# Merged score groups, sliding values read at once, and float32 modulation sums in a decoder layer on one core

## The chip, the cores and the metric

The kernel runs on one core of one Trainium2 chip. A core has five engines that run their own instruction streams side by side and wait for each other by semaphores: PE (TensorE, matrix multiplication into PSUM), DVE (VectorE), ACT (ScalarE), POOL (GpSimd) and SP (SyncE, which here only issues DMAs). In the profile PEld is PE's loading of weights. PSUM has eight banks of 128 partitions by 512 float32 values, and each score or product has to be read out of its bank before the bank is used again.

The metric is the device time of one execution in microseconds, as the median of several executions. The profile is of one further execution; its own time and its span stand in the table below.

## The reference

One decoder layer on a sequence of 512 rows of 1024 values, in float32, cut to what matters here:

```python
mod = cs @ w_ada[l] + b_ada[l]                  # cs = silu(c), one row of 1024; mod has 6 rows of 1024
shift1, scale1, gate1, shift2, scale2, gate2 = split(mod, 6)
h = _rmsnorm(x, norm1_g[l]) * (1.0 + scale1) + shift1
qa, ka, va, qd, kd, vd, ga, gd = split(h @ w_in[l], points)
out_a = _sliding_window_attention(qa, ka, va, sinks, slopes)   # 8 heads, 2 key heads, window 128, blocks of 128
out_d = _diff_attention(qd, kd, vd, lam, ...)                  # 4 heads, softmax 0 minus lam times softmax 1, causal
merged = sigmoid(ga) * (out_a @ w_branch_swa[l]) + sigmoid(gd) * (out_d @ w_branch_diff[l])
x = x + gate1 * (merged @ w_out[l])
h2 = _rmsnorm(x, norm2_g[l]) * (1.0 + scale2) + shift2
x = x + gate2 * _conv_ffn(h2, ...)
return _rmsnorm(x, final_g)
```

The change touches three places: the scores of the two kinds of attention, the moment at which a sliding head's values are read out, and the last four rows of `mod` (gate1, shift2, scale2, gate2).

## The kernel before

**Precision.** A large product is made of three matmuls of fp32r operands (`mm3`, L118 to L121): each operand is split into a high part, rounded by ACT (`split`, L115), and a low part, the difference, made by DVE (L116); high times high, high times low and low times high are summed in one bank. `evac` does the same on the way out of a bank: ACT writes the high part (L430, or L433 with a scale), DVE the low part (L431, L434).

**PE's order is written out.** PE's instructions run in the order of the program text (`manual_schedule`, for PE alone). ACT, DVE, POOL and SP are ordered by a planner that simulates the program; where the text has `high_priority`, an instruction is taken as soon as it can run. So the order on those engines can change where only PE's text was touched.

**The fill.** Between the pieces of attention PE works on projections. `fill(n)` (L491) takes n steps from a list of units, a unit being one output block of 128 columns of a weight (q, k and v of a differential head, or a gate, or a branch), and a step three matmuls of 512 columns. The counts stand in `SWA_FILL` and `DIFF_FILL` (L37, L38). A weight comes by a DMA into one of four raw buffers (tag "raw", L105), is split, and then frees its raw buffer. `fill` also counts ticks: things put off by `after(n, ...)` run n ticks later, and every eighth tick the generator `ada_rows` goes one step.

**PSUM.** Two banks "f" for the fill, three "s" for scores, two "t" for transposes and other short uses, one "v" for the values of a head (L90 to L103).

**Sliding heads**, in four pairs i (heads i and i+4; j is 0 or 1). `swa_scores` (L532) makes the scores of four blocks n of 128 queries against 128 keys (block 0) or 256, two blocks at a time; the two j use the two halves of the array's rows, six matmuls for a block (`mm3_rows`, L126). DVE adds the window's bias and takes the maximum (L559). `swa_softmax` makes nm from the maxima (L570) and exponentials on ACT (es at L571, st at L574), and DVE divides (L582). `swa_transpose` (L593) turns the probabilities in the two "t" banks; ACT copies them out as pT (L595). `swa_values` (L604) multiplies by the values, the two j in the two halves of the array's columns, and `evac` (L609) writes outa with the planner's ordinary priority. Within a round i, the first two blocks of pair i+1 come ahead of the fill, the other two behind the second transpose of pair i, and the softmax of i+1 after one more fill.

**Differential heads**, in 16 steps s (head h, block n of 128 queries against (n+1) × 128 keys). `diff_scores` (L648 to L677) makes two maps m in the two halves of the rows; DVE adds the bias and takes the maximum (L673). Then nm (L685), exponentials (L687), the difference of the maps (L690 to L693), the transpose td (L702) and its `evac` to aTh and aTl (L705, L430, L431). `diff_values` (L709) makes od once in a head. Which scores are made at a step stands in `nxt`: blocks 0 and 1 together, 2 and 3 alone.

**Turning the values.** The values of a differential head come out transposed as vT (L632) and are turned by PE 13 ticks later (`turn`, pv, L637) into a "t" bank.

**The modulation rows.** `ada_rows` (L743) sums each of eight half rows (4 rows, 2 halves) over the input in blocks of two times 128: SP loads ra (L750) into a raw buffer, DVE multiplies by cs and sums into `arow` (L755 for the first, L757 for the other seven). All eight half rows use the one buffer "sq2". The sum over partitions follows on PE: `arow` is split into arh and arl, and a product with an all-ones 128x128 matrix puts the sum into every row of pr (L766, L767). ACT copies row 0 back into the same buffer (L769), and POOL's DMA puts it into DRAM (L770).

Of the kernel before, what the change touches and what calls it, by code (L numbers as in the profile page):

```python
# [53 lines left out]
def kernel(  # L54
# [78 lines left out]
    warm = cpool.tile([P, 1], F32, name="warm")  # L133
    nc.vector.memset(warm, 0.0)
    nc.scalar.activation(warm, warm, AF.Exp)
    onesr = cpool.tile([P, P], F32R, name="onesr")
    nc.vector.tensor_copy(onesr, ones)
    mhalf = cpool.tile([P, 4], F32, name="mhalf")
    nc.gpsimd.memset(mhalf, -0.5)
    qsc = cpool.tile([P, 4], F32, name="qsc")  # L140
# [388 lines left out]
    class Pair:  # L529
        pass  # L530

    def swa_scores(i, n0):  # L532
        if n0 == 0:
            c = pairs[i] = Pair()
            c.mx, c.nm, c.lsum, c.es = (
                ap.tile([P, 2, NT], F32, tag=t, bufs=2, name=f"{t}{i}") for t in ("mx", "nm", "lsum", "es")
            )
            c.sb = [ap.tile([P, 2, P], F32, tag="st0", bufs=2, name=f"st{i}_0")]
            c.sb += [ap.tile([P, 2, 256], F32, tag="st", bufs=ST, name=f"st{i}_{n}") for n in range(1, NT)]
            c.pT = []  # L540
        c = pairs[i]
        sps = [sbank(f"sw{i}_{n0}_{j}", (P, 2, 256)) for j in range(2)]
        for n in (n0, n0 + 1):
            w = P if n == 0 else 2 * P
            k0 = max(0, n - 1) * P
            qs, ks = slice(n * P, (n + 1) * P), slice(k0, k0 + w)
            mm3_rows([
                (
                    sps[j][:, n - n0, :w],
                    [qa[64 * j : 64 * j + 64, i, b, qs] for b in range(2)],  # L550
                    [ka[64 * j : 64 * j + 64, b, ks] for b in range(2)],
                )
                for j in range(2)
            ])
        for n in (n0, n0 + 1):
            w = P if n == 0 else 2 * P
            for j in range(2):
                with tc.high_priority(offset=HP):
                    c.last = nc.vector.tensor_tensor_reduce(  # L559
                        c.sb[n][:, j, :w], sps[j][:, n - n0, :w], dsw[:, 256 - w : 256], 1.0, -3e38, ALU.add, ALU.max,  # L560
                        c.mx[:, j, n : n + 1],
                    )

# [34 lines left out]
    def swa_values(i):  # L598
        o = vbank(f"oa{i}")
        for kb in (0, 2, 1, 3):  # L600
            w = P if kb == 3 else 2 * P
            for j in range(2):
                rows = slice(64 * j, 64 * j + 64)
                nc.tensor.matmul(  # L604
                    o[rows, kb * P : kb * P + w], va[:, kb, rows],
                    pairs[i].pT[j][:, kb * 256 : kb * 256 + w],
                    start=kb == 0, stop=kb == 3, tile_position=(0, 64 * j),
                )
        evac(outa[0][:, i], outa[1][:, i], o)  # L609


    heads = {}
# [35 lines left out]
    def diff_scores(*ss):  # L648
        ops = []
        for s in ss:  # L650
            h, n = divmod(s, NT)
            t = heads[h]
            w = (n + 1) * P
            if n == 0:
                firsts[h] = [sbank(f"sd{h}_{m}", (P, 2, 256)) for m in range(2)]
            sps = [firsts[h][m][:, n, :w] if n < 2 else sbank(f"sd{h}_{n}_{m}")[:, :w] for m in range(2)]
            mm3_rows([
                (
                    sps[m],
                    [t[64 * m : 64 * m + 64, b, n * P : (n + 1) * P] for b in range(2)],  # L660
                    [t[64 * m : 64 * m + 64, 2 + b, :w] for b in range(2)],
                )
                for m in range(2)
            ])
            ops.append((s, sps, w))
        for s, sps, w in ops:
            h, n = divmod(s, NT)
            mx = ap.tile([P, 2], F32, tag="dmx", bufs=3, name=f"dmx{h}_{n}")
            pm = []
            for m in range(2):  # L670
                st = ap.tile([P, w], F32, tag="st", bufs=ST, name=f"sd{h}_{n}_{m}")
                with tc.high_priority(offset=HP):
                    nc.vector.tensor_tensor_reduce(  # L673
                        st, sps[m], ddf[:, 512 - w : 512], 1.0, -3e38, ALU.add, ALU.max, mx[:, m : m + 1]
                    )
                pm.append(st)
            scored[s] = mx, pm  # L677
# [65 lines left out]
    def ada_rows():  # L743
        for idx in range(4):
            for hf in range(2):
                c0 = (2 + idx) * D + hf * S
                ac = big.tile([P, S], F32, tag="sq2", name=f"arow{idx}{hf}")
                for k in range(0, KT, 2):
                    r = raw_tile([P, 2, S], f"ra{idx}{hf}_{k}")
                    nc.sync.dma_start(r, wada[k * P : (k + 2) * P, c0 : c0 + S].rearrange("(a p) n -> p a n", p=P))  # L750
                    with tc.high_priority(offset=HP // 2) if tick[0] > ADA_EASY else ExitStack():
                        for a in range(2):
                            cc = cs[:, k + a : k + a + 1]
                            if k + a == 0:
                                nc.vector.tensor_scalar_mul(ac, r[:, a], cc)  # L755
                            else:
                                nc.vector.scalar_tensor_tensor(ac, r[:, a], cc, ac, ALU.mult, ALU.add)  # L757
                    yield
                ah = big.tile([P, S], F32R, tag="g2b0", name=f"arh{idx}{hf}")
                al = big.tile([P, S], F32R, tag="g2b1", name=f"arl{idx}{hf}")  # L760
                split(ah, al, ac)
                after(ADA_LAG, lambda idx=idx, hf=hf, ac=ac, ah=ah, al=al: ada_spread(idx, hf, ac, ah, al))

    def ada_spread(idx, hf, ac, ah, al):
        pr = tbank(f"pr{idx}{hf}")
        nc.tensor.matmul(pr, onesr, ah, start=True, stop=False)  # L766
        nc.tensor.matmul(pr, onesr, al, start=False, stop=True)  # L767
        row = ac[0:1, :]
        nc.scalar.copy(row, pr[0:1, :])  # L769
        nc.gpsimd.dma_start(mod_rows[idx : idx + 1, hf * S : (hf + 1) * S], row)  # L770


    pair_w = {}
# [29 lines left out]
    add_head(0)  # L803
    add_head(1)
    fill(SWA_FILL[0])
    swa_scores(0, 0)
    with tc.issue_after(pairs[0].last.ins):
        fill(SWA_FILL[1])
        swa_scores(0, 2)
    with tc.issue_after(pairs[0].last.ins):  # L810
        swa_softmax(0)
        fill(1)
# [2 lines left out]
        fill(SWA_FILL[2] - 1)  # L815
    for i in range(SWA_PAIRS):
        more = i + 1 < SWA_PAIRS
        if more:
            swa_scores(i + 1, 0)
        fill(SWA_FILL[3])  # L820
        swa_transpose(i, 0)
        fill(SWA_FILL[4])
        swa_transpose(i, 1)
        if more:
            swa_scores(i + 1, 2)
        fill(SWA_FILL[5])
        if more:
            swa_softmax(i + 1)
# [14 lines left out]
    for s in range(4 * DIFF_HEADS):  # L843
# [4 lines left out]
            add_gate_a(2)  # L848
            add_gate_a(3)
        fill(DIFF_FILL[1])  # L850
        nxt = {0: (), 1: (s + 1,), 2: (s + 1,), 3: (s + 1, s + 2)}[n] if s < 15 else ()
        if nxt:
            diff_scores(*nxt)
        fill(DIFF_FILL[2])
# [932 lines left out]
```

## Time and profile before

| | us |
|---|---|
| median of 3 runs | 706.98 (706.82 to 708.46) |
| the profiled execution's own time | 708.24 |
| its span in the trace | 705.4 |
| PE busy / DVE busy / ACT busy in the span | 685.0 / 578.4 / 383.9 |
| sliding attention on PE, first score group to last values | 61.5 to 116.8 |
| differential attention on PE, first scores to last values | 116.8 to 217.0 |
| modulation sums on PE (pr), first and last | 108.2 and 293.1 |

How to read it: a row of a timeline has the start in us from the span's beginning, the duration, the engine, the line, the operation, what it writes and reads by tile names, the partitions and elements, and how many equal instructions were merged into the row. A bracket gives the idle time ahead of it and whose event ended it. Matmuls overlap in the records (a record has 0.39 us where the next one starts 0.23 later), so prices on PE are taken from start to start. Rows on ACT and DVE overlap a little too.

### The profile page before, as it was taken

To read this page: it belongs to the slowest core of one execution; us is meant where nothing else is said; L and a number is where in the kernel's file an instruction comes from. 1 tells how busy PE (TensorE), PEld (TensorE's weight loads), DVE (VectorE), ACT (ScalarE), POOL (GpSimd) and SP (SyncE) were. 2 spreads that over 40 slices of the span, in tenths; PEclk is the share of its full clock that TensorE was granted. 3 is DMA by queue.
4 is the path that set the end of the run, shared out by engine and by line. 5 is a ranking of instruction groups with operands and counts; after the bars stand their busy time and mean duration, and the time that the engine had idled before them with its cause. 6 is when DMAs were issued, how large, how long until landed. Compare 5 with 4: busy or idle time off the path is not lost. (4 is left out here: it accounts for less than half of the span.)

```text
span 705.4 us, 11197 instructions
## 1 busy us (share of the span) xinstructions
PE 685.0 (97%) x4155; PEld 597.1 (85%) x4155; DVE 578.4 (82%) x1107; ACT 383.9 (54%) x676; POOL 82.2 (12%) x100
## 2 busy tenths in 40 slices
PE   6999999999999999999999999999999999999994
PEld 6777777777787888888889999999999999888884
DVE  5998968788985766773579899888888999979996
ACT  3646766545543333431468656555555666656664
POOL 3000000000011000000030111111101102530300
PEclk9999999999999999999999999999999999999998
DMA  9983624263543774529617888786979748996803
GB/s 311 302 262 98 201 61 154 67 199 90 170 153 100 262 214 142 186 93 288 187 33 148 197 199 204 177 209 182 208 204 230 164 143 204 197 200 191 158 0 119
DMA packets 115861, 121.80 MB, mean 173 GB/s; under 512 B 4415, under 2 KB 93280, under 8 KB 115808
## 3 DMA queue, kind: packets, MB, share of 16 engines
q1 hardware_dynamic: 96894, 95.09, 42.7%
q0 software_dynamic: 18720, 25.73, 21.6%
q8 instruction: 32, 0.52, 0.3%
q10 hardware_dynamic: 194, 0.28, 0.1%
q14 instruction: 21, 0.17, 0.1%
HBM read 118.97 MB, written 2.11 MB: 172 GB/s over the span
## 5 line engine op out<-in xcount | busy, mean ns | idle before, releaser
L1126 PE MATMUL up<-t,m_whi 128*128 128x256 f32 x528 | 96.1, 283 | 0.0
L1126 PEld LDWEIGHTS up<-t,m_whi 128*128 128x128 f32 x528 | 82.3, 192 | 0.0
L1126 PE MATMUL up<-t,m_wlo 128*128 128x256 f32 x264 | 74.7, 283 | 0.1
L1126 PE MATMUL up<-bh,p_wlo 128*128 128x256 f32 x232 | 65.7, 284 | 0.7 <-DVE p_wlo L1069 0.7
L1126 PE MATMUL up<-bh,p_whi 128*128 128x256 f32 x232 | 65.6, 283 | 0.0
L1126 PE MATMUL up<-bl,p_whi 128*128 128x256 f32 x232 | 65.6, 283 | 0.0
L1126 PEld LDWEIGHTS up<-t,m_wlo 128*128 128x128 f32 x264 | 50.6, 192 | 0.3 <-DVE m_wlo L1069 0.3
L1126 PEld LDWEIGHTS up<-bh,p_wlo 128*128 128x128 f32 x232 | 44.5, 192 | 1.1 <-DVE p_wlo L1069 1.1
L1126 PEld LDWEIGHTS up<-bh,p_whi 128*128 128x128 f32 x232 | 44.5, 192 | 0.0
L1126 PEld LDWEIGHTS up<-bl,p_whi 128*128 128x128 f32 x232 | 44.5, 192 | 0.0
L757 DVE SCALAR_TENSOR_TENSOR arow<-ra,cs,arow 128x512 f32<-128x512 f32 x56 | 41.9, 747 | 2.6 <-DMA ra<-in_w_ada_dram 1.8
L1037 POOL DMA_DIRECT2D s<-in_w_up_dram x21 | 27.0, 1361 | 142.9 <-DMA s<-in_w_up_dram 78.0
L1069 DVE TENSOR_TENSOR m_wlo<-s,m_whi 128x1024 fp32r<-128x1024 f32 x31 | 37.7, 1217 | 2.0 <-ACT m_whi L1065 2.0
L1065 ACT CAST m_whi<-s 128x1024 fp32r<-128x1024 f32 x31 | 32.5, 1047 | 9.4 <-DVE s L1059 5.9
L1126 PE MATMUL up<-t,p_whi 128*128 128x256 f32 x176 | 32.2, 283 | 0.0
L687 ACT ACTIVATE sd<-sd,dmx 128x128 f32<-128x128 f32 (+3 forms) x32 | 17.8, 556 | 23.2 <-DVE dmx L685 15.9
L175 POOL TENSOR_TENSOR r<-ms,mhalf 128x1 f32<-128x1 f32 (+1 forms) x16 | 13.2, 828 | 144.7 <-DVE ms L173 74.0
L1126 PEld LDWEIGHTS up<-t,p_whi 128*128 128x128 f32 x176 | 27.4, 192 | 0.2 <-issue 0.2
L1133 ACT ACTIVATE gT<-a,cv 128x512 f32<-128x512 f32 x22 | 17.7, 813 | 17.6 <-DVE a L1168 17.3
L770 POOL DMA_DIRECT2D mod_rows<-arow x8 | 4.3, 540 | 193.7 <-ACT arow L769 193.5
L1065 ACT CAST p_whi<-wa 128x1024 fp32r<-128x1024 f32 x18 | 18.7, 1041 | 12.0 <-PE up L1126 7.2
L1126 PE MATMUL up<-t,p_wlo 128*128 128x256 f32 x88 | 24.9, 283 | 0.0
(478 smaller groups left out, 2073.0 us busy)
## 6 DMA issues: line engine op xcount, KB each, us to landing
ra<-in_w_ada_dram SPq DMA_DIRECT2D x32, 512.0 KB, 4.2
wa<-in_w_up_dram SPq DMA_DIRECT2D x22, 512.0 KB, 4.6
s<-in_w_up_dram SPq DMA_DIRECT2D x21, 512.0 KB, 5.1
s<-in_w_up_dram POOLq DMA_DIRECT2D x21, 512.0 KB, 7.0
adaw<-in_w_ada_dram SPq DMA_DIRECT2D x16, 512.0 KB, 4.9
w<-in_w_in_dram SPq DMA_DIRECT2D x12, 512.0 KB, 4.1
a<-in_w_up_dram SPq DMA_DIRECT2D x11, 512.0 KB, 4.8
b<-in_w_down_dram SPq DMA_DIRECT2D x10, 512.0 KB, 4.7
```

Source lines behind the costliest of these rows:

```text
L175: nc.gpsimd.tensor_tensor(r0, ms, mhalf[:, :n], ALU.pow)
L687: nc.scalar.activation(pm[m], pm[m], AF.Exp, bias=mx[:, m : m + 1], scale=slope, accum_out=lsum[:, m : m + 1])
L757: nc.vector.scalar_tensor_tensor(ac, r[:, a], cc, ac, ALU.mult, ALU.add)
L770: nc.gpsimd.dma_start(mod_rows[idx : idx + 1, hf * S : (hf + 1) * S], row)
L1037: nc.gpsimd.dma_start(dst, upblock(*blk), accum_op=ALU.add)
L1065: nc.scalar.copy(W[J, name][0], R[J, SRC[name]])
L1069: nc.vector.tensor_sub(lo, R[J, SRC[name]], hi.bitcast(F32))
L1126: nc.tensor.matmul(o[u], w[:, k, cu], b[:, k], start=name in ("p1", "m5", "p2") and k == 0 and x == 0, stop=k == 3 and x == 2, skip_group_ ...
L1133: nc.scalar.activation(grow(j), av[J][:, u], AF.Identity, bias=cv[:, 66 + j : 67 + j], scale=cv[:, 44 + j : 45 + j])
```

## The change

Five edits.

1. The scores of sliding pairs 1 to 3 are made in one group of four blocks, which stands after the fill of the round and ahead of the first transposition; pair 0 keeps its two groups. Four blocks need four banks: the three "s" and, for the second pair of blocks of j = 1, the bank "v".
2. The scores of blocks 2 and 3 of a differential head are made in one group, at the step of block 1; the bank of block 3's second map is "v". With the first edit there are 13 groups of scores instead of 20.
3. The `evac` of a sliding pair's values is at high priority.
4. Of the sums of the modulation rows, the second half of each row has the buffer "g2b1", the first keeps "sq2"; the copied row has a tile of its own ("g2b0").
5. The sum over partitions is made of four float32 matmuls, each of 128 columns of `arow` into its own quarter of the array's columns (32 wide), without the split into arh and arl. ACT copies all of pr (128x128), and the DMA takes rows 0, 32, 64 and 96.

```diff
-    onesr = cpool.tile([P, P], F32R, name="onesr")
-    nc.vector.tensor_copy(onesr, ones)
...
-    def swa_scores(i, n0):
-        if n0 == 0:
+    def swa_scores(i, blocks):
+        if 0 in blocks:
...
-        sps = [sbank(f"sw{i}_{n0}_{j}", (P, 2, 256)) for j in range(2)]
-        for n in (n0, n0 + 1):
+        sps = {
+            (g, j): vbank(f"sw{i}_{g}_{j}").rearrange("p (a q) -> p a q", a=2)
+            if len(blocks) == NT and (g, j) == (1, 1) else sbank(f"sw{i}_{g}_{j}", (P, 2, 256))
+            for g in sorted({n // 2 for n in blocks}) for j in range(2)
+        }
+        for n in blocks:
...
-        evac(outa[0][:, i], outa[1][:, i], o)
+        with tc.high_priority(offset=HP):
+            evac(outa[0][:, i], outa[1][:, i], o)
...
-            sps = [firsts[h][m][:, n, :w] if n < 2 else sbank(f"sd{h}_{n}_{m}")[:, :w] for m in range(2)]
+            sps = [
+                firsts[h][m][:, n, :w] if n < 2 else (vbank if n + m == 4 else sbank)(f"sd{h}_{n}_{m}")[:, :w]
+                for m in range(2)
+            ]
...
-                ac = big.tile([P, S], F32, tag="sq2", name=f"arow{idx}{hf}")
+                ac = big.tile([P, S], F32, tag=("sq2", "g2b1")[hf], name=f"arow{idx}{hf}")
...
-                ah = big.tile([P, S], F32R, tag="g2b0", name=f"arh{idx}{hf}")
-                al = big.tile([P, S], F32R, tag="g2b1", name=f"arl{idx}{hf}")
-                split(ah, al, ac)
-                after(ADA_LAG, lambda idx=idx, hf=hf, ac=ac, ah=ah, al=al: ada_spread(idx, hf, ac, ah, al))
-
-    def ada_spread(idx, hf, ac, ah, al):
-        pr = tbank(f"pr{idx}{hf}")
-        nc.tensor.matmul(pr, onesr, ah, start=True, stop=False)
-        nc.tensor.matmul(pr, onesr, al, start=False, stop=True)
-        row = ac[0:1, :]
-        nc.scalar.copy(row, pr[0:1, :])
-        nc.gpsimd.dma_start(mod_rows[idx : idx + 1, hf * S : (hf + 1) * S], row)
+                after(ADA_LAG, lambda idx=idx, hf=hf, ac=ac: ada_spread(idx, hf, ac))
+
+
+    def ada_spread(idx, hf, ac):
+        pr = tbank(f"pr{idx}{hf}", (P, P))
+        for g in range(4):
+            gs = slice(32 * g, 32 * g + 32)
+            nc.tensor.matmul(
+                pr[gs], ones[:, gs], ac[:, g * P : (g + 1) * P], start=True, stop=True, tile_position=(0, 32 * g)
+            )
+        row = big.tile([P, P], F32, tag="g2b0", name=f"row{idx}{hf}")
+        nc.scalar.copy(row, pr)
+        nc.gpsimd.dma_start(
+            mod_rows[idx, hf * S : (hf + 1) * S].rearrange("(g n) -> g n", g=4), row[0:P:32]
+        )
...
-    swa_scores(0, 0)
+    swa_scores(0, (0, 1))
...
-        swa_scores(0, 2)
+        swa_scores(0, (2, 3))
...
+        fill(SWA_FILL[3])
         if more:
-            swa_scores(i + 1, 0)
-        fill(SWA_FILL[3])
+            swa_scores(i + 1, range(NT))
         swa_transpose(i, 0)
         fill(SWA_FILL[4])
         swa_transpose(i, 1)
-        if more:
-            swa_scores(i + 1, 2)
         fill(SWA_FILL[5])
...
-        nxt = {0: (), 1: (s + 1,), 2: (s + 1,), 3: (s + 1, s + 2)}[n] if s < 15 else ()
+        nxt = (s + 1, s + 2) if n % 2 and s < 15 else ()
```

More of the change, by code (lines that the diff above doesn't have):

```diff
@@ L548, in swa_scores @@
                 (
-                    sps[j][:, n - n0, :w],
+                    sps[n // 2, j][:, n % 2, :w],
                     [qa[64 * j : 64 * j + 64, i, b, qs] for b in range(2)],
@@ L554, in swa_scores @@
             ])
-        for n in (n0, n0 + 1):
+        for n in blocks:
             w = P if n == 0 else 2 * P
@@ L559, in swa_scores @@
                     c.last = nc.vector.tensor_tensor_reduce(
-                        c.sb[n][:, j, :w], sps[j][:, n - n0, :w], dsw[:, 256 - w : 256], 1.0, -3e38, ALU.add, ALU.max,
+                        c.sb[n][:, j, :w], sps[n // 2, j][:, n % 2, :w], dsw[:, 256 - w : 256], 1.0, -3e38, ALU.add, ALU.max,
                         c.mx[:, j, n : n + 1],
```

## The prediction

> **What bounds the kernel now.** I read the page's engine totals first, then its chain of waits, then the busy times by stretch, then TensorE's waits.
>
> ```profile
> span 705.4 us, 11197 instructions
> PE 685.0 (97%) x4155; PEld 597.1 (85%) x4155; DVE 578.4 (82%) x1107; ACT 383.9 (54%) x676; POOL 82.2 (12%) x100
> PE 41%; DVE 5%; issue 1%; ACT 1%; POOLq 0%; DVEq 0%; ACTq 0%
> ```
>
> PE is busy for 97% of the span, and it leads the chain of waits with 41%; no other engine holds more than 5% of that chain. So the time moves only if PE's own instructions get fewer or shorter, or if PE waits more or less. In the stretches that the change touches (columns: busy us and instructions of each engine, then PE's granted clock):
>
> ```profile
> 60.00:140.00 80.00, 80.00 (x497) 61.47 (x496) 63.86 (x207) 49.78 (x138) 1.21 (x2) 1.00 0.37 113
> 140.00:200.00 60.00, 58.69 (x316) 46.97 (x316) 52.40 (x143) 33.31 (x79) 3.91 (x4) 1.00 0.49 142
> ```
>
> PE has no gap from 60 to 140 us and 1.3 us of gaps in the next 60. DVE has 63.86 busy of 80 and 52.40 of 60: little slack, so a shift in DVE's order can reach PE. The clock is 1.00, so I scale nothing by it. What PE waits for in the attention phase is small:
>
> ```profile
> PE td L702 <- DVE sd L693: 1.6, 3, 1.1
> PE od L120 <- DVE aTl L431: 0.5, 1, 0.5
> ```
>
> **The merged score groups.** A score group (L126) uses half the rows of the array, and PE pays for going into this form and out of it. The rows show the price:
>
> ```profile
> 125.74 0.40 PE L121 MATMUL pA<-outah,wba_l 128*128 128x512 f32 x1
> 126.07 0.79 PE L126 MATMUL sd<-qkv 64*128 64x384 f32 x6
> 126.79 0.50 PE L119 MATMUL pA<-outah,wba_h 128*128 128x512 f32 x1
> 127.13 0.39 PE L120 MATMUL pA<-outal,wba_h 128*128 128x512 f32 x1
> ```
>
> From the start of the last plain matmul (125.74) to the second plain one after the group (127.13) are 1.39 us. Two plain steps would be 0.46: a fp32r matmul of 512 columns starts every 0.23 us, as the rows of 134.45, 134.68 and 134.91 further down show. So the group costs 0.93. Its six matmuls are three pairs side by side in the two halves; 384 columns at 0.23 per 512 are 0.17, three times 0.52. The rest, 0.41, is paid per group, and not per matmul. The same sum for a sliding group:
>
> ```profile
> 68.61 0.39 PE L121 MATMUL pk<-hThA,w_l 128*128 128x512 f32 x1
> 68.93 0.96 PE L126 MATMUL sw<-ka,qa 64*128 64x128 f32 x12
> 69.81 0.50 PE L119 MATMUL pk<-hThA,w_h 128*128 128x512 f32 x1
> 70.15 0.39 PE L120 MATMUL pk<-hTlA,w_h 128*128 128x512 f32 x1
> ```
>
> That is 1.54 − 0.46 = 1.08, less 0.52 for three pairs of 128 and of 256 columns: 0.56. Part of it belongs to the twelve short matmuls and stays, so I take the 0.40 of the first sum for each. Seven groups go: three for the sliding pairs 1 to 3, four for blocks 2 and 3 of the differential heads. 7 × 0.40 = **−2.8 us** (−2.5 to −3.9 with 0.36 and 0.56).
>
> [...]
>
> **The rows of the modulation, on PE.** Now each of eight half rows is summed over the partitions by two plain matmuls:
>
> ```profile
> 134.45 0.39 PE L766 MATMUL pr<-arh,onesr 128*128 128x512 f32 x1
> 134.68 0.39 PE L767 MATMUL pr<-arl,onesr 128*128 128x512 f32 x1
> 134.91 0.40 PE L119 MATMUL pA<-outah,wba_h 128*128 128x512 f32 x1
> ```
>
> 0.46 each, with no change of form. The new one is four float32 matmuls of 32 output rows and 128 columns, each in its own quarter of the array's columns. The trace has no such shape; the nearest is the sliding values, float32 in two halves of the columns:
>
> ```profile
> 77.89 0.39 PE L121 MATMUL pw<-hThA,w_l 128*128 128x512 f32 x1
> 78.21 1.73 PE L604 MATMUL oa<-pT,va 128*64 128x256 f32 x16
> 79.87 0.50 PE L119 MATMUL pw<-hThA,w_h 128*128 128x512 f32 x1
> 80.21 0.40 PE L120 MATMUL pw<-hTlA,w_h 128*128 128x512 f32 x1
> ```
>
> Sixteen records for eight matmuls: a float32 matmul passes twice. The two halves run together, so there are six passes of 256 columns and two of 128, 1,792 columns in the 1.66 us from 78.21 to 79.87: 0.93 ns a column, or 0.12 us for 128. The group costs 2.32 − 0.46 = 1.86, of which about 0.35 goes for the change of form (0.09 ahead, 0.11 behind, and the slow first pass and drain between). For the new sum: two passes of 128 are 0.24 if all four quarters run together, 0.48 if two do, 0.95 if they go one by one. With 0.35: 0.59, 0.83 and 1.30, against 0.46. The row's two halves ran together, so the first is nearest: +0.13 × 8 = **+1.1 us** (0 to +6.7).
>
> **What goes from ACT and DVE.** Gone are eight casts and eight subtractions of 512 columns, and the copy of a row shrinks. The subtraction is the first row here, 0.60 us to the next; the rest are prices for below (a weight's low part 1.13, maxima of 256 columns 0.345 each, so four 1.38):
>
> ```profile
> 87.66 0.68 DVE L116 TENSOR_TENSOR arl<-arow,arh 128x512 fp32r<-128x512 f32 x1
> 88.26 1.22 DVE L116 TENSOR_TENSOR w_l<-w,w_h 128x1024 fp32r<-128x1024 f32 x1
> 89.39 0.42 DVE L559 CUSTOM_DVE_ANT_0 st<-sw,dsw 128x256 f32<-128x256 f32 x1
> ...
> 90.77 0.35 DVE L570 TENSOR_SCALAR nm<-mx,nsink 128x4 f32<-128x4 f32 x2
> ```
>
> None of it is on PE's path by itself: zero, apart from the order it gives DVE. Separate buffers let the next row be summed earlier, from about 85 us instead of 113; that puts L757 between other DVE work (its group, and the time from issue to landing of the blocks ra that it reads):
>
> ```profile
> L757 DVE SCALAR_TENSOR_TENSOR arow<-ra,cs,arow 128x512 f32<-128x512 f32 x56 | 41.9, 747 | 2.6 <-DMA ra<-in_w_ada_dram 1.8
> DMA to landing us min/median/max: 3.6/4.2/5.2
> ```
>
> **The new wait.** Before, all eight maxima of pair i+1 were ready only after transposes 0 and 1 of pair i, so ACT took the copies of these (L595) first and the softmax afterwards:
>
> ```profile
> 91.09 0.30 ACT L571 ACTIVATE es<-nm,sink 128x4 f32<-128x4 f32 x1 [2.00 <-DVE nm L570]
> 93.15 0.28 ACT L571 ACTIVATE es<-nm,sink 128x4 f32<-128x4 f32 x1
> ...
> 97.01 1.05 ACT L115 CAST wga_h<-wga 128x1024 fp32r<-128x1024 f32 x1 [1.25 <-issue]
> 97.97 0.59 ACT L433 ACTIVATE qkv<-pq 128x512 fp32r<-128x512 f32 x1
> 98.45 0.96 ACT L595 COPY pT<-tp 128x512 f32<-128x512 f32 x2
> 100.55 0.97 ACT L595 COPY pT<-tp 128x512 f32<-128x512 f32 x2 [1.13 <-PE tp L593]
> 103.53 0.30 ACT L571 ACTIVATE es<-nm,sink 128x4 f32<-128x4 f32 x1
> ```
>
> In the changed program's order on ACT, es and one or two exponentials of pair i+1 stand ahead of the copies of transpose 1 of pair i. ACT takes its work in order, so those copies now wait for nm of the next pair. PE needs them for the next use of a "t" bank (two buffers) and for the values. For pairs 1 and 2 the copies still come about in time (+0.15). For pair 3 they don't, because of what stands ahead of nm on DVE. My working starts at nm of pair 2, an estimate of 89.05: oa's cast now directly follows the exponentials of pair 1, and its low part is done at about 83.0; then come three steps of the modulation sum (1.9 together, from the 0.75 of the row above less the overlap with the next), a low part 0.60, a weight's low part 1.13 and eight maxima, 2.4.
>
> - ACT: two softmax halves at 2.06 (91.09 to 93.15) with the two copies (0.97) among them end at 94.3; a copy and a cast of 512 columns at 0.48 (97.97 to 98.45), a cast of 1,024 at 0.96 (97.01 to 97.97), and DVE's low part at 1.13 give 97.3.
> - This releases a raw buffer, and only then SP issues the next modulation block (ra), which lands 4.2 us later: 101.5. DVE meanwhile does a low part 1.13, qkv's 0.6 and four maxima, two of them narrower, 1.1, and stands at 100.1 before that block's L757, with four maxima and nm of pair 3 behind it in the queue.
> - L757 0.67, four maxima 1.38 and nm 0.15: 103.7; es and an exponential 0.6, the copy 0.48: 104.8.
>
> PE wants the bank for turning head 0's values:
>
> ```profile
> 102.41 0.60 PE L637 MATMUL pv<-ident,vT 128*128 128x128 f32 x4
> ```
>
> There it would be at 102.41 − 3 × 0.40 + 0.15 = 101.4. The stall is **+3.4 us**; with the quickest and slowest landing of these blocks (3.6 and 5.2) 2.8 and 4.4; with a block that is there in time 2.0; and 0 if the exponentials turn out behind the copies. PE can't make it up: all of its later work comes that much later.
>
> **The waits of the differential phase.** The longest is ended by DVE:
>
> ```profile
> 144.96 0.30 PE L702 MATMUL td<-ident,sd 128*128 128x128 f32 x1 [1.14 <-DVE sd L693]
> 215.53 0.50 PE L120 MATMUL od<-aTl,qkv 128*128 128x512 f32 x1 [0.47 <-DVE aTl L431]
> ```
>
> PE comes to td some 2.3 us later, DVE less so, since its subtractions are gone but two L757 wait for their blocks: 1.14 becomes 0.55 (0 to 1.6); the two other td waits (1.6 − 1.1 = 0.5) go. **−1.1 us** (−1.6 to +0.5). At 215.53 a weight's low part (1.13) now stands ahead of aTl instead of behind it, after a transposition that no longer waits: 0.47 becomes 1.0, **+0.5 us** (0 to +0.8). The bank that the merged groups borrow from the values costs nothing: by the same count its reader, the low part of oa (83.0), is done 0.9 us ahead of the score matmul that wants it; if it were late, PE would wait at most for that 0.6 us step.
>
> **The sum.** −2.8 + 1.1 + 3.4 + 0.15 − 1.1 + 0.5 = **+1.25 us**. On the profiled execution's span, 705.4 becomes 706.6, and with the 2.84 us around it (708.24 − 705.4) 709.5. That execution is 1.26 above the median of 706.98, so the median comes to 708.2.
>
> **The rivals.**
> 1. The copies aren't held up: the new order on ACT harms nothing as the maxima come early, being merged and moved ahead. For it: the merged group is over before the transposes start. Against it: the block ahead of nm, which can't be issued before 97.3. Then the 3.5 go: 706.98 − 2.3 = 704.7.
> 2. The four quarters of the modulation sums don't run together: slower by PE's own work. At two at a time +3.0 instead of +1.1, one by one +6.7, together with the stall 710.1 to 713.9. It decides from about 0.7 us for one sum on (eight times 0.24 is the whole of 2 us). For it: no row shows four together; each has two passes that need weights of their own, and four in a row are more than the two that 78.21 shows. Against: in 78.21 the halves don't slow each other.
> 3. The stall is there, but the block comes in time (2.0): 706.8, no change.
> 4. The change doesn't do what it says: PE's pair of groups costs as much together as apart, since the 0.40 belongs to the matmuls. Then +2.8: 711.0. Against it are the 0.34 and 0.10 around the group, which merging removes.
>
> [...]
>
> **How the numbers follow.** A measurement of this kernel can tell about 0.3% from no change, 2.1 us: below 704.9 is faster, above 709.1 slower. Forecast 0.38, rival 1 0.23, rival 2 0.17, rival 3 0.15, rival 4 0.07. Around the forecast lie ±1.5 us: a third of it is above 709.1. Faster: half of rival 1, a fifth of rival 3 and a part of the forecast where sums fall low, 0.24. Slower: rivals 2 and 4 and a third of the forecast, 0.36. The same: 0.40. The range: from rival 1, 704.2, to the two-at-a-time case with a slow landing, 711.2; the forecast's own is 706.6 to 709.8.
>
> **What would show it.** Right: a wait of PE at pv (its L637) of 2 to 4.4 us near 101 us, ended by ACT's pT, with nm and an ra block behind it in the chain; 13 score groups with about 1.8 us for a sliding and 1.6 for a differential one; PE 0.55 to 0.65 from the first modulation matmul to the next plain one; td's longest wait around 0.5 and od's around 1. Wrong: no wait at pv, a modulation sum above 0.8, or a gap of PE at the first score matmul of a group, which would be the borrowed bank.

## The result and the profile after

| | median us | runs | own time and span of the profiled execution |
|---|---|---|---|
| before | 707.02 (706.69 to 708.46) | 10 | 708.24, 705.4 |
| after | 709.55 (707.96 to 711.68) | 10 | 709.33, 707.4 |

The ratio is 1.0031, with a 95% interval of 1.0018 to 1.0044: the change makes the kernel slower by some 2.2 us. One of the six executions of only_diff, below, took 2766 us at a full clock and is left out of its figures. Line numbers of the changed kernel are shifted: its L763 is L757 of before, L640 is L637, L606 is L604, L597 is L595, L573 is L571, L572 is L570, L708 is L702, L699 is L693, L428 and L429 are L430 and L431.

The page of the changed kernel, and what PE and DVE waited for (us in total, times, longest):

```profile
span 707.4 us, 11251 instructions
PE 684.4 (97%) x4203; PEld 595.8 (84%) x4203; DVE 572.1 (81%) x1098; ACT 376.0 (53%) x668; POOL 82.3 (12%) x100
```
```profile
PE pv L640 <- ACT pT L597: 3.4, 1, 3.4
...
PE od L120 <- DVE aTl L429: 0.9, 1, 0.9
...
PE td L708 <- DVE sd L699: 0.6, 1, 0.6
...
PE od L119 <- ACT aTh L428: 0.3, 1, 0.3
```
```profile
DVE arow L763 <- DMA ra<-in_w_ada_dram: 21.1, 12, 4.2
```

PE is busy for as long as before; what is new is one wait of 3.4 us at pv. And DVE, which hardly waited for modulation blocks before (1.8 us for this line, and 5.7 us at the first block of a row for the last row's transfer out of the one buffer), waits 21.1 us for them, with other work queued behind. PE's own rows show the wait, and something more behind it:

```profile
101.32 0.40 PE L121 MATMUL pk<-hThA,w_l 128*128 128x512 f32 x1
105.14 0.66 PE L640 MATMUL pv<-ident,vT 128*128 128x128 f32 x4 [3.42 <-ACT pT L597]
105.55 0.48 PE L119 MATMUL pk<-hThA,w_h 128*128 128x512 f32 x1
...
107.23 0.63 PE L121 MATMUL pk<-hThA,w_l 128*128 128x512 f32 x1
107.65 0.63 PE L119 MATMUL pk<-hThB,w_h 128*128 128x512 f32 x1
108.08 0.63 PE L120 MATMUL pk<-hTlB,w_h 128*128 128x512 f32 x1
```

The last three start every 0.43 us, where this matmul started every 0.23. The busy times by stretch have the reason (columns: the stretch, its length, PE's busy time and instructions, PE's granted clock, share and GB/s of the DMAs):

```profile
104.00:106.00 2.00, 0.86 (x6) 1.00 0.15 20
106.00:108.00 2.00, 2.00 (x7) 0.56 0.84 261
108.00:110.00 2.00, 2.00 (x9) 0.58 0.64 220
110.00:112.00 2.00, 2.00 (x16) 1.00 0.07 27
```

Half the clock (0.50) for 3.4 us, from 106.3 to 109.7: the two middle rows reach a little beyond it on either side. From 106.37 to 111.01 the same instructions at full pace would take some 1.5 us less: five steps of 0.43 instead of 0.23, the change of form 0.2 longer, the values of pair 2 1.94 instead of 1.66.

Upstream, the chain is the one that was drawn. SP issues the block ra at 97.63, released by DVE's low part of a weight. On DVE:

```profile
101.57 0.75 DVE L763 SCALAR_TENSOR_TENSOR arow<-ra,cs,arow 128x512 f32<-128x512 f32 x1 [1.13 <-DMA ra<-in_w_ada_dram]
...
103.62 0.35 DVE L572 TENSOR_SCALAR nm<-mx,nsink 128x4 f32<-128x4 f32 x2
```

and on ACT:

```profile
98.63 0.97 ACT L597 COPY pT<-tp 128x512 f32<-128x512 f32 x2 [0.94 <-PE tp L595]
103.94 0.30 ACT L573 ACTIVATE es<-nm,sink 128x4 f32<-128x4 f32 x1 [4.34 <-DVE nm L572]
...
104.53 0.94 ACT L597 COPY pT<-tp 128x512 f32<-128x512 f32 x2
```

ACT does nothing for 4.34 us, with the copies that PE needs queued behind es. The block was forecast to land at 101.5 and does at 101.57; nm was forecast for 103.7 and comes at 103.62.

The same order on ACT costs something a round earlier, where the list of waits doesn't show it. The copies of pair 1's second transposition stand behind es of pair 2 and start at 90.37, just as PE begins with the values of pair 1:

```profile
90.38 2.33 PE L606 MATMUL oa<-pT,va 128*64 128x256 f32 x16
92.64 0.50 PE L119 MATMUL pq<-hThA,w_h 128*128 128x512 f32 x1
```

The sixteen matmuls take 2.26 us instead of 1.66, since two of their weight loads wait for pT (0.41 and 0.17); a merged row hides such gaps.

The prices on PE, start to start, first a merged sliding group with a transposition behind it and one alone, then a merged differential group, then a modulation sum:

```profile
95.96 0.39 PE L121 MATMUL pk<-hThA,w_l 128*128 128x512 f32 x1
96.28 1.67 PE L126 MATMUL sw<-ka,qa 64*128 64x128 f32 x24
97.88 0.98 PE L595 MATMUL tp<-ident,st 128*128 128x128 f32 x7
98.62 0.48 PE L119 MATMUL pk<-hThA,w_h 128*128 128x512 f32 x1
98.93 0.39 PE L120 MATMUL pk<-hTlA,w_h 128*128 128x512 f32 x1
...
99.86 0.39 PE L121 MATMUL pk<-hThA,w_l 128*128 128x512 f32 x1
100.09 0.93 PE L595 MATMUL tp<-ident,st 128*128 128x128 f32 x7
100.77 0.48 PE L119 MATMUL pk<-hThA,w_h 128*128 128x512 f32 x1
101.09 0.40 PE L120 MATMUL pk<-hTlA,w_h 128*128 128x512 f32 x1
```
```profile
130.04 0.39 PE L121 MATMUL pA<-outah,wba_l 128*128 128x512 f32 x1
130.36 1.49 PE L126 MATMUL sd<-qkv 64*128 64x384 f32 x12
131.78 0.50 PE L119 MATMUL pA<-outah,wba_h 128*128 128x512 f32 x1
132.12 0.40 PE L120 MATMUL pA<-outal,wba_h 128*128 128x512 f32 x1
```
```profile
112.27 0.39 PE L121 MATMUL pw<-hThA,w_l 128*128 128x512 f32 x1
112.59 0.43 PE L772 MATMUL pr<-arow,ones 128*32 128x128 f32 x8
112.94 0.50 PE L119 MATMUL pw<-hThA,w_h 128*128 128x512 f32 x1
113.28 0.39 PE L120 MATMUL pw<-hTlA,w_h 128*128 128x512 f32 x1
```

Two plain steps are 0.46. The transposition alone costs 1.23 − 0.46 = 0.77, so the sliding group costs 2.97 − 0.46 − 0.77 = 1.74. The two that it replaces cost 1.08 and 1.10 (the second stood behind a transposition, with it 2.33 from 86.44 to 88.77, less 0.46 and 0.77): 0.44 less. The differential group costs 2.08 − 0.46 = 1.62; the two that it replaces cost 0.93 and, for block 3, 1.09 (1.55 from 131.04 to 132.59, less 0.46): 0.40 less. A modulation sum costs 1.01 − 0.46 = 0.55; eight records in 0.43 us, at a cost near the 0.59 of the forecast and far from 0.83, mean that the four quarters run together. The records say the same: they start in two fours, at 112.59 to 112.61 and at 112.72 to 112.74.

### The profile page after: what moved, and what is told of

It reads as the page before. It is cut to its first block, busy times and chain, and to the rows that moved or that the text cites. A ratio compares the mean times of both kernels' runs of the same rounds, so it can differ in the third digit from the quotient of the medians.

```text
span 707.4 us, 11251 instructions
## 1 busy us (share of the span) xinstructions
PE 684.4 (97%) x4203; PEld 595.8 (84%) x4203; DVE 572.1 (81%) x1098; ACT 376.0 (53%) x668; POOL 82.3 (12%) x100
## 5 line engine op out<-in xcount | busy, mean ns | idle before, releaser
L763 DVE SCALAR_TENSOR_TENSOR arow<-ra,cs,arow 128x512 f32<-128x512 f32 x56 | 41.9, 749 | 21.7 <-DMA ra<-in_w_ada_dram 21.1
L777 POOL DMA_DIRECT2D mod_rows<-row x8 | 4.9, 612 | 211.4 <-ACT row L776 211.4
L693 ACT ACTIVATE sd<-sd,dmx 128x128 f32<-128x128 f32 (+3 forms) x32 | 17.7, 554 | 19.4 <-DVE dmx L691 19.4
```

Of the source, the lines that this page charges most:

```text
L693: nc.scalar.activation(pm[m], pm[m], AF.Exp, bias=mx[:, m : m + 1], scale=slope, accum_out=lsum[:, m : m + 1])
L777: nc.gpsimd.dma_start(mod_rows[idx, hf * S : (hf + 1) * S].rearrange("(g n) -> g n", g=4), row[0:P:32])
```

## The experiments

The ratio of each is to the kernel before, timed beside it on the same chip; every interval is 95%.

**Only the order of the copies** (copies_first). Pair 3's softmax is queued behind pair 2's copies on ACT; nothing else differs from the changed kernel.

```diff
-                nc.scalar.copy(pt[:, b * 512 : b * 512 + wb], tp[:, :wb])
+                c.copied = nc.scalar.copy(pt[:, b * 512 : b * 512 + wb], tp[:, :wb])
...
         if more:
-            swa_softmax(i + 1)
+            with tc.issue_after(pairs[i].copied.ins) if i == 2 else ExitStack():
+                swa_softmax(i + 1)
```

> The changed kernel, but on ACT the softmax of sliding pair 3 is queued behind the copies of pair 2's second transpose. Theory (the order on ACT holds those copies until nm of pair 3, and PE's idle time then costs clock): no wait of PE at pv above 0.3 us, granted clock 1.00 from 100 to 115 us, nm of pair 3 as late as before (about 103.6); 709.5 less 3.4 of wait and about 1.6 of clock, with up to 1.5 given back at td and od: 704.5 to 706.5. Rival (the merged groups or the modulation sums cost PE itself): 708.5 to 710.5, since these are unchanged.

Measured: 705.68, ratio 0.9977 (0.9967 to 0.9987). PE has no wait at pv. Here are its busy time and clock (1.00) in the stretch where the changed kernel lost most, and what is left of its waits in the differential phase:

```profile
60.00:140.00 80.00, 79.58 (x511) 61.07 (x510) 67.60 (x215) 47.92 (x137) 1.35 (x2) 1.00 0.47 142
```
```profile
PE od L120 <- DVE aTl L429: 0.9, 1, 0.9
PE td L708 <- DVE sd L699: 0.7, 1, 0.7
```

So this one order on ACT is worth 3.9 us with the clock behind it, and with it undone the rest of the change gains: the theory holds, and the merged groups and the sums don't cost what the rival says. nm of pair 3 comes at 103.11, about as late as before. Note td: 0.7 although PE comes early again.

**One buffer for the modulation rows** (one_buffer).

```diff
-                ac = big.tile([P, S], F32, tag=("sq2", "g2b1")[hf], name=f"arow{idx}{hf}")
+                ac = big.tile([P, S], F32, tag="sq2", name=f"arow{idx}{hf}")
```

> The changed kernel, but both halves of a modulation row use one buffer again; no modulation block then stands ahead of pair 3's nm on DVE, while es and two exponentials still stand ahead of the copies on ACT. Theory (the 3.4 us wait has two parts: the order on ACT, some 2.0, and the block that comes late, some 1.4): wait at pv 1.5 to 2.2 us, clock 1.00 after it, 706.3 to 708.0. If the order on ACT alone makes the wait: 3 us or more and a reduced clock, 709 to 710. If the block alone makes it: under 0.5 us, 704.5 to 706.

Measured: 710.97, ratio 1.0051 (1.0035 to 1.0067). PE's waits:

```profile
103.23 0.66 PE L640 MATMUL pv<-ident,vT 128*128 128x128 f32 x4 [1.35 <-ACT pT L597]
```
```profile
145.39 0.30 PE L708 MATMUL td<-ident,sd 128*128 128x128 f32 x1 [1.01 <-DVE sd L699]
```
```profile
187.32 0.52 PE L708 MATMUL td<-ident,sd 128*128 128x128 f32 x3 [2.22 <-DVE drs L183]
```

The wait at pv goes from 3.4 to 1.35, so the 3.4 has both parts, the order on ACT and the late block, the block's somewhat the larger (2.0 expected to stay, 1.35 did). But the time was missed: it doesn't fall, though its interval overlaps that of the changed kernel (1.0018 to 1.0044). td now waits 3.6 in all instead of 0.6, and this trace loses another 1.2 us between 220 and 367 us, half of it in a wait at th that the change doesn't touch. So the second buffer, which makes the wait at pv 2.1 us longer, saves 3.0 us of waits at td.

**The merged sliding scores alone** (only_swa): the kernel before with `swa_scores(i + 1, range(NT))` ahead of the transposes, the borrowed bank, and the early `evac` of the values.

```diff
+        fill(SWA_FILL[3])
         if more:
-            swa_scores(i + 1, 0)
-        fill(SWA_FILL[3])
+            swa_scores(i + 1, range(NT))
         swa_transpose(i, 0)
         fill(SWA_FILL[4])
         swa_transpose(i, 1)
-        if more:
-            swa_scores(i + 1, 2)
```

> The kernel before with the merged sliding scores and the early reading of sliding values alone. Theory: three groups fewer, -1.2; es and two exponentials of pair 3 still ahead of the copies, but no modulation block on DVE, so a wait at pv or oa of 0.5 to 1.5 us; 705.8 to 707.5, clock 1.00 between 60 and 140 us. Rival (merging itself costs, by the borrowed bank or the order): 708 or more. If no wait is left: 705.0 to 705.8.

Measured: 707.41, ratio 1.0000 (0.9990 to 1.0009); a wait at pv of 1.1, td 2.0 instead of 1.6. As expected: the three groups' 1.3 us are paid back, most of it at pv.

**The new modulation sums alone** (only_sums): the kernel before with the two buffers and the sums in quarters.

```diff
-                split(ah, al, ac)
-                after(ADA_LAG, lambda idx=idx, hf=hf, ac=ac, ah=ah, al=al: ada_spread(idx, hf, ac, ah, al))
...
+                after(ADA_LAG, lambda idx=idx, hf=hf, ac=ac: ada_spread(idx, hf, ac))
```

> The kernel before with the new modulation sums and their buffers alone. Theory: no wait at pv (the copies are ahead of the softmax on ACT), eight sums at 0.55 instead of 0.46, +0.7, and some change of the td and od waits, -1 to +0.5: 706.4 to 708.2. Rival (the sums in quarters of the columns are what makes the changed kernel slow): 709 or more.

Measured: 710.00, ratio 1.0033 (1.0019 to 1.0048). The time is the rival's, its reason isn't: a sum still costs 0.55, 0.7 us in eight. The rest is td:

```profile
PE td L700 <- DVE sd L691: 3.6, 5, 1.1
```
```profile
122.55 1.54 DVE L755 SCALAR_TENSOR_TENSOR arow<-ra,cs,arow 128x512 f32<-128x512 f32 x2 [2.66 <-DMA ra<-in_w_ada_dram]
```

DVE waits for a block, in order, just ahead of the steps that make sd. This block stands ahead of the first of the five waits (0.42 us at 125.35); the others I haven't followed. I had expected the td waits to shrink here.

**The merged differential scores alone** (only_diff), with the bank "v" for block 3's second map.

```diff
-        nxt = {0: (), 1: (s + 1,), 2: (s + 1,), 3: (s + 1, s + 2)}[n] if s < 15 else ()
+        nxt = (s + 1, s + 2) if n % 2 and s < 15 else ()
```

> The kernel before with the merged differential scores alone. Theory: four groups fewer at 0.41, -1.6, and td and od waits within 1 us of before's 2.1: ratio to before 0.9965 to 0.999. Rival (what merging saves is lost to later maxima, or to the borrowed bank): ratio 0.999 to 1.003, with td or od waits 1 us longer or a wait at a score matmul.

Measured: 712.43, ratio 1.0073 (1.0053 to 1.0092). Wrong by far: the two longest waits at td are 2.59 and 2.84, and ahead of the first DVE stands idle, not for a block but for the row's own transfer out of the one buffer:

```profile
147.18 0.30 PE L705 MATMUL td<-ident,sd 128*128 128x128 f32 x1 [2.59 <-DVE sd L696]
```
```profile
141.13 0.49 DVE L758 TENSOR_SCALAR arow<-ra,cs 128x512 f32<-128x512 f32 x1 [3.00 <-DMA mod_rows<-arow]
141.54 0.28 DVE L676 CUSTOM_DVE_ANT_0 sd<-sd,ddf 128x128 f32<-128x128 f32 x1
```
```profile
162.00:165.00 3.00, 0.38 (x4) 0.41 (x5) 2.47 (x4) 0.00 (x0) 0.00 (x0) 1.00 0.01 4
165.00:168.00 3.00, 3.00 (x18) 2.10 (x18) 0.56 (x1) 0.48 (x1) 0.00 (x0) 0.64 0.60 179
168.00:171.00 3.00, 3.00 (x12) 2.29 (x11) 1.41 (x10) 0.00 (x0) 0.00 (x0) 0.50 0.00 0
```

The maxima (L676) are queued behind the 3.00. No such transfer stands ahead of the second wait (2.84, ending at 164.6): there a weight's low part of 1.1 us, at 162.73, stands on DVE between the last two steps of sd, as it does ahead of the 2.22 in one_buffer; why DVE is late by then stays open. Behind this second wait the clock falls to 0.50 here too.

**The other combinations.** The kernel before with both merges and its own sums (old_sums):

```diff
-                after(ADA_LAG, lambda idx=idx, hf=hf, ac=ac: ada_spread(idx, hf, ac))
...
+                split(ah, al, ac)
+                after(ADA_LAG, lambda idx=idx, hf=hf, ac=ac, ah=ah, al=al: ada_spread(idx, hf, ac, ah, al))
```

> The kernel before with both merges and the early reading of sliding values, but with its own modulation sums and their one buffer. Theory (in the differential phase the merges need the second row buffer, since with one DVE waits some 3 us for the row's transfer ahead of the maxima): a wait at pv of about 1.1 as in only_swa, td waits of 3 to 5.5 us as in only_diff; -2.8 + 1.1 + 2 to 4 and some lost clock: ratio to before 1.001 to 1.008. Rival (the 5.4 us of td waits in only_diff belong to its place in time and go when PE comes 1 us later): td waits below 2, ratio 0.997 to 0.9995.

Then the differential merges and the sums, without the sliding merges and the early reading of the values (diff_sums):

```diff
+        if more:
+            swa_scores(i + 1, 0)
         fill(SWA_FILL[3])
-        if more:
-            swa_scores(i + 1, range(NT))
...
-        with tc.high_priority(offset=HP):
-            evac(outa[0][:, i], outa[1][:, i], o)
+        evac(outa[0][:, i], outa[1][:, i], o)
```

> The kernel before with the merged differential scores and the new modulation sums, its sliding scores as before. Theory: no wait at pv, -1.6 for four groups, +0.7 for eight sums, td and od waits together 1 to 2.5 us (2.1 before): ratio to before 0.997 to 1.0005. Rival (the merged differential scores cost by themselves, as only_diff might be read): td waits of 4 us or more, ratio 1.004 or more.

And the sliding merges and the sums, without the differential merges (swa_sums):

```diff
-        nxt = (s + 1, s + 2) if n % 2 and s < 15 else ()
+        nxt = {0: (), 1: (s + 1,), 2: (s + 1,), 3: (s + 1, s + 2)}[n] if s < 15 else ()
```

> The changed kernel with differential scores as before. Theory: the 3.4 us wait at pv is there, since it needs only the merged sliding scores and the early modulation block, and the clock falls behind it: 3.0 to 3.8 us and 0.5 to 0.7 for some us; -1.2 + 0.7 + 3.4 + 1.6 and td waits of 0 to 2 less the 1.6 of before: ratio to before 1.002 to 1.007. Rival (the wait at pv needs the differential merges too): no wait above 1.5 there, ratio below 1.001.

All eight combinations side by side (waits of PE in us, of the profiled execution; od is both of its waits; the sliding merges have the early reading of the values with them, which was never tried alone):

| sliding merges | differential merges | new sums | ratio | interval | pv | td | od |
|---|---|---|---|---|---|---|---|
| no | no | no | 1 | | 0 | 1.6 | 0.5 |
| yes | no | no | 1.0000 | 0.9990 to 1.0009 | 1.1 | 2.0 | 0.5 |
| no | yes | no | 1.0073 | 1.0053 to 1.0092 | 0 | 5.4 | 1.4 |
| no | no | yes | 1.0033 | 1.0019 to 1.0048 | 0 | 3.6 | 0.4 |
| yes | yes | no | 1.0067 | 1.0050 to 1.0085 | 1.1 | 5.6 | 1.5 |
| no | yes | yes | 0.9997 | 0.9983 to 1.0010 | 0 | 1.1 | 1.2 |
| yes | no | yes | 1.0087 | 1.0074 to 1.0101 | 3.3 | 3.3 | 0.4 |
| yes | yes | yes | 1.0031 | 1.0018 to 1.0044 | 3.4 | 0.6 | 1.1 |

Three things are read off. td is short only where the differential merges and the new sums come together; each alone makes it longer by 2 to 4 us. And the wait at pv needs the sliding merges, and is 3.3 to 3.4 with the new sums and 1.1 without. The waits at od are 1.1 to 1.5 with the differential merges and 0.4 to 0.5 without, whatever else is changed. The waits at pv came out as expected in all three, and the times of old_sums and diff_sums too. In swa_sums td waits 3.3 us, against 0 to 2 expected; it came out slower than its range by 1.2 us, and its profiled execution shows no fall of the clock, against what I expected there (columns: the stretch, its length, busy time and instructions of PE, PEld, DVE, ACT and POOL, then clock, share and GB/s of the DMAs, as in only_diff):

```profile
104.00:106.00 2.00, 0.54 (x5) 0.54 (x6) 1.93 (x7) 1.74 (x6) 0.00 (x0) 1.00 0.02 5
106.00:108.00 2.00, 2.00 (x11) 1.47 (x9) 1.14 (x5) 2.00 (x10) 0.00 (x0) 1.00 0.77 251
```

**Work put into the wait** (filler). This kernel does 14 matmuls more than the reference needs; nothing uses them.

```diff
             def turn():
+                if h == 0:
+                    for _ in range(14):
+                        nc.tensor.matmul(qbank[1], hT[0][0][:, 0:P], hT[0][0], start=True, stop=True)
                 pv = tbank(f"pv{h}")
```

> The changed kernel, with 14 extra matmuls of 512 columns (3.2 us) into a bank already read out, just ahead of pv: PE works through the wait, on nothing that is used. Theory (the idle time itself lowers the granted clock): pv still starts near 105.1 us, the rest of the wait there is under 0.5 us, clock 1.00 from 100 to 115 us, and the time is shorter than the changed kernel's by what the slow matmuls cost, about 1.6: 707.3 to 708.6. Rival (the clock fell for another reason, or in that one profile only): clock 0.5 to 0.7 after 106 us again, 709 to 710.5.

Measured: 707.82, ratio 1.0014 (1.0003 to 1.0024), against 1.0031 for the changed kernel: about 1.2 us less with more work. The stretches:

```profile
100.00:105.00 5.00, 4.92 (x26) 3.90 (x25) 4.00 (x15) 1.35 (x5) 0.00 (x0) 1.00 0.41 147
105.00:110.00 5.00, 5.00 (x33) 3.59 (x33) 3.48 (x14) 4.77 (x18) 0.00 (x0) 1.00 0.70 205
```

PE's clock stays at 1.00. The mean clocks of the executions, 0.993 to 0.997 here and 0.988 to 0.994 in the changed kernel, hardly overlap; with the waits compared in the last section I take it as shown that it was the idle 3.4 us that lowered the clock here, though a wait of 3.28 us didn't in swa_sums, above. The gain of 1.2 us is less certain: the two intervals overlap a little (1.0018 and 1.0024), and the profiled execution, with 709.31 the slowest of the eleven, has the same span as the changed kernel's, 707.4.

**The modulation steps queued later** (late_sums).

```diff
-                for k in range(0, KT, 2):
-                    r = raw_tile([P, 2, S], f"ra{idx}{hf}_{k}")
-                    nc.sync.dma_start(r, wada[k * P : (k + 2) * P, c0 : c0 + S].rearrange("(a p) n -> p a n", p=P))
+                def sums(k, r, ac=ac):
                     with tc.high_priority(offset=HP // 2) if tick[0] > ADA_EASY else ExitStack():
...
+                for k in range(0, KT, 2):
+                    r = raw_tile([P, 2, S], f"ra{idx}{hf}_{k}")
+                    nc.sync.dma_start(r, wada[k * P : (k + 2) * P, c0 : c0 + S].rearrange("(a p) n -> p a n", p=P))
                     yield
+                    with tc.issue_after(recent[0].ins) if recent else ExitStack():
+                        sums(k, r)
```

> The changed kernel, but the multiplications of a modulation block are queued one step of the generator later than its transfer and behind the last maximum of the scores on DVE; ACT then has the copies of pair 2 ahead of pair 3's softmax. Theory (DVE loses 21 us by waiting, in order, for modulation blocks, and what is queued behind reaches PE late): DVE's wait for ra below 6 us, no wait at pv, td waits below 0.6 together; ratio to before 0.994 to 0.998. Rival (the raw buffers, held longer, delay weights): a wait of PE for weights of 1 us or more, ratio 0.999 or more.

Measured: 714.54, ratio 1.0111 (1.0093 to 1.0130), the slowest of all. pv is free, and DVE waits 10.3 us for blocks at this line instead of 21.1 (under 6 expected; at the line of a row's first block 7.4 instead of 3.6). But the sums are now late for PE (2.7 us at pr), od waits 2.2 for aTl, and a gate's matmul 1.7 (pga, ended by ACT's ta). Waiting less on DVE was no end in itself; the rival's direction was right, but none of these waits is ended by a weight, so its reason isn't shown.

**A version that beats both** the kernel before and the changed one (best1): copies_first, and the split of the sixth gate's weight behind aTh and aTl of the last differential block:

```diff
-            nc.scalar.copy(hi, src)
-            nc.vector.tensor_sub(lo, src, hi.bitcast(F32))
+            done[0] = nc.scalar.copy(hi, src), nc.vector.tensor_sub(lo, src, hi.bitcast(F32))
...
+        def load_gate():
+            if j != 5:
+                return load_cols(win, COL_GA + j * P, f"wga{j}")
+            with tc.issue_after(done[0][0].ins), tc.issue_after(done[0][1].ins):
+                return load_cols(win, COL_GA + j * P, f"wga{j}")
```

> The kernel copies_first, and the split of the sixth gate's weight is queued behind the last differential block's aTh and aTl on ACT and DVE. Theory (the od waits of 0.25 and 0.88 us are these two steps ahead of aTh and aTl): both gone, -1.1 against copies_first; ratio to before 0.995 to 0.9972. Rival (the waits move to the gate's own matmuls, which then lack their weight): 0.997 to 0.9985 and a new wait at pga.

Measured: 703.98, ratio 0.9957 (0.9943 to 0.9971); od waits 0.2. Its interval just meets that of copies_first (0.9967 to 0.9987). With the copy of pr at high priority as well (best2):

```diff
-        nc.scalar.copy(row, pr)
+        with tc.high_priority(offset=HP):
+            nc.scalar.copy(row, pr)
```

> The kernel best1 with ACT's copy of the summed row at high priority. Theory (the 0.4 us wait of a transpose for this copy, near 110 us, goes and nothing else moves): ratio to before 0.9945 to 0.9965. Rival (the copy stands ahead of exponentials and delays td): ratio above 0.9965 with a longer td wait.

Measured: 704.33, ratio 0.9964 (0.9950 to 0.9979): no gain that the intervals can tell, and the wait that it was meant for is still 0.5.

## Why the prediction was right, and where it was off

| term | forecast | measured |
|---|---|---|
| seven groups fewer | −2.8 | −2.9 |
| eight modulation sums | +1.1 | +0.7 |
| wait at pv | +3.4 | +3.4 |
| values of pair 1 | +0.15 | +0.6 |
| td, 1.64 to 0.55 | −1.1 | −1.05 |
| od, 0.47 to 1.0 | +0.5 | +0.66 |
| clock behind the wait | not in the sum | +1.5 |
| th, 0.7 to 0 | not in the sum | −0.7 |
| sum | +1.25 | +2.2 |

The span rose by 2.0, and the ratio says 2.2 (1.3 to 3.1). The row th is a wait behind the attention that the change doesn't touch; it comes and goes between the traces (0 in copies_first, 1.5 in best2). That the forecast of 708.2 came within 1.4 us of the 709.55 measured is partly luck: what it left out or mis-sized, +1.5, +0.45, −0.7 and −0.4, partly cancels.

The sign and the mechanism were right. The merges save what the rows promised, and rival 4 is out. The four quarters run together, and rival 2 is out; the change of form was taken at 0.35 and is nearer 0.3 (of the 0.35, 0.15 lay already in the price of a pass, as this was taken from all of the 1.66 us). The wait at pv came at the place, with the length and through the steps that were worked out, so rivals 1 and 3 are out; copies_first and one_buffer show that both links, the order on ACT and the block ahead of nm on DVE, are needed for its length. The same order on ACT was taken as nearly harmless for pair 1 (+0.15); the values of that pair took 0.6 longer here as in copies_first, filler and swa_sums, and 0.2 longer in one_buffer.

The step that fell short is "PE can't make it up: all of its later work comes that much later". It stopped at the wait; behind it, the granted clock was 0.50 from 106.3 to 109.7 us, and I had set the clock aside because it was 1.00 in a kernel without such a wait. How many executions of the changed kernel meet the fall, the record doesn't tell. Five of the ten have a mean clock of 0.994 and a median of 708.4, the other five 0.992 or less and 710.3. But 3.4 us at half the clock take 0.002 off the mean wherever they lie, and the first 60 us alone had a clock of 1.00 in diff_sums, 0.97 in the kernel before and 0.94 in only_swa, none of which falls at pv. That the changed kernel is near the 708.2 of the forecast where the clock doesn't fall is likely, then, and not shown.

The reason given for td was wrong, though its size was right. It was to shrink because PE comes later and DVE is rid of the subtractions. In copies_first PE isn't late and td is 0.7; in only_sums the subtractions are gone and td is 3.6. What the table of combinations and one_buffer (td 3.6, with both merges and the sums in quarters) show is that the merged differential scores and the second buffer have to come together. Why is shown only in part: without the buffer DVE waits for the row's transfer ahead of the maxima (3.00 us in only_diff), which is behind one of the two long waits there; without the merges it waits for blocks ahead of sd, seen at one of the five waits of only_sums. Why the latter is harmless once the scores are merged, I haven't followed through.

## What to carry to other kernels

Where a planner orders an engine that takes its work in order, look at what stands ahead of the instruction that the bottleneck waits for: here one early exponential cost 3.4 us, and putting it behind two copies turned a loss of 0.3% into a gain of 0.2%. Price a wait of TensorE of some 3 us with the lower clock that may come with it, not only with its length: here 1.5 us for the wait of 3.42, and the clock fell at waits of 2.71, 2.84 and 2.87 too. Look into merged rows too: a gap inside a group of matmuls stands in no list of PE's waits. And test the parts of a change together as well as alone: the differential merges lose 0.7% alone and the new sums 0.3%, but together nothing that the interval can tell (0.9997).

## What was unexpected

The length of a wait alone doesn't decide on the clock. It fell at waits shorter than the 3.42 us of the changed kernel, at 2.84 us in only_diff and at 2.71 and 2.87 in old_sums, and stayed at 1.00 behind 3.28 in swa_sums, 2.59 in only_diff and 2.22 in one_buffer. In late_sums, whose two longest waits in these phases are 2.7 us (pr) and 2.2 (od), it was 0.96 from 160 to 200 us and 0.98 from 220 to 330.

The stretches of half clock have lengths in common. In the changed kernel they lie at 14.10 to 17.51 us and at 106.26 to 109.67: each lasts 3.41 us, and they begin 92.16 us apart, 27.0 times that. Worked out from the clocks by stretch, the one of only_diff lasts some 6.8 us (from 165.8) and those of old_sums some 3.4 and 10.3 (from 147.0 and 164.1): two, one and three times 3.41, and the two of old_sums begin 17.1 apart, five times. In the 3.41 us ahead of its fall PE stood idle for 2.30 us in the changed kernel, some 2.2 in only_diff, and some 2.3 and 2.0 in old_sums, where the second fall comes before the wait is over. Divide the time from 20 to 690 us into such periods, laid from the fall on in both directions: no other one in the changed kernel has more than 1.13 us of idle time, and in the kernel before, laid from its own half clock at 14.24, where the clock is 1.00 all through, none has more than 1.02. It is an estimate of mine from these four falls that the place of a wait in such periods counts beside its length. Where the waits of swa_sums and one_buffer lie in theirs is not shown, and no run was made to test it.

The single profiles also differ where the kernels don't. The first score group starts between 61.0 us (diff_sums) and 62.7 (only_diff), and the wait at th lies between 0 and 1.5 us, so that spans of single profiles can't be compared to better than a microsecond or two.
